# A two-layer hybrid diffusion backbone on one core: the convolution's output product gets its weights and two token operands in another way, and the layer heads order their norm and token sums anew

## The chip, the cores and the metric

The kernel runs on one core of a Trainium2 chip. The metric is the device time of one execution in microseconds, here the median of several runs. Before the change it is 2621.95 us (three runs, 2616.47 to 2628.95). A core has a matrix engine (TensorE, PE in the profile; its weight loads are shown as PEld), VectorE (DVE), ScalarE (ACT), GpSimd (POOL) and a queue engine SyncE (SP) that issues transfers. Each engine works through its own queue in order.

## The reference

Two layers over 1024 latent tokens of width 1024, with 256 context tokens that only the first layer reads. Layer 0 mixes tokens by bidirectional retention, layer 1 by a gated convolution of three taps; a SwiGLU block with 2816 hidden features follows each mixer. Every sub-layer is normed and modulated ahead and gated behind. Cut to what matters here (all of it float32):

```python
def rms_norm(x, gain=None):
    y = x * lax.rsqrt(jnp.mean(x * x, axis=-1, keepdims=True) + EPS)
    return y if gain is None else y * gain

def modulate(x, shift, scale):
    return x * (1 + scale) + shift

def conv_mixer(h, w_in, w_conv, w_out):
    b_gate, c_gate, xv = jnp.split(h @ w_in, 3, axis=-1)
    return (b_gate * short_conv(c_gate * xv, w_conv)) @ w_out

def swiglu(h, w1, w3, w2):
    return (jax.nn.silu(h @ w1) * (h @ w3)) @ w2

for i in range(2):
    sh1, sc1, g1, sh2, sc2, g2 = ada_params(c, ada_w[i], ada_b[i])
    ax = modulate(rms_norm(hx, norm_mix[i]), sh1, sc1)
    yx = retention_mixer(ax, ac, ...) if i == 0 else conv_mixer(ax, ...)
    hx = hx + g1 * yx
    fx = modulate(rms_norm(hx, norm_ffn[i]), sh2, sc2)
    hx = hx + g2 * swiglu(fx, ffn_w1[i], ffn_w3[i], ffn_w2[i])
return rms_norm(hx, final_norm)
```

## The kernel before, in words

**Precision.** Every large operand is held in two float32r parts, high and low. `split` makes them: ScalarE copies (rounds) the high part (L132, or L127 when the sign is turned), VectorE subtracts it from the source to get the low part (L133, or L128). `mm3` multiplies high by low, low by high and high by high into one bank of PSUM: three matmuls of 128 x 512 (L137 to L139). A pair of parts is one unit tile, from a pool of 38 that raw weight tiles of the same size share; single token tiles come from a pool of twelve (`ttile`) and one of twelve more (`ttile2`).

**Seven products.** Each weight matrix is multiplied by the tokens in a scheme of Strassen's kind (Winograd's form): weight and tokens are cut in halves both ways, and seven products of sums take the place of eight. Tokens are in two halves of 512 (`tb`), features in halves of four tiles of 128. x11, x12, x21, x22 are the quarters of the token matrix: first digit the half of the features, second digit the half of the tokens. Product 1 needs x11, product 2 x21, product 3 x22; products 5, 6, 7, 4 need sums: x12 - x11 and so on, in a chain. The tokens' sums are made in place; in the layers that widen, the norm's step already gives x12 and x21 the opposite sign, so that every step of the chain is an addition.

**Units.** In the layers that widen (`up_layer`, `winograd_products`) a unit is one product of one block of 128 output features: four feature tiles times three matmuls, twelve in all. In the layers that narrow (`down`) a unit is one product and one contraction tile for four output tiles, twelve matmuls again. The widening layers here are the feed-forward of layer 0, the convolution's input, the feed-forward of layer 1; the narrowing ones are the retention's output, the two feed-forward outputs and the convolution's output. The latter has four contraction tiles (`nh == 4`), hence 28 units, in the order of products 1, 5, 6, 3, 7, 4, 2. A widening layer starts with four blocks at once: product 1 of all four, product 2 of all four, then 5, 6, 7, 3, 4; after them the blocks follow one by one. Its first units, up to the start of product 5, are called its head.

**Order.** Work off TensorE is written as small functions in a list, `hooks`. After each unit `unit_done` takes one or more from the front; an entry `nothing` is a pause, which ends the turn. `until` takes hooks until an operand exists. What is written this way is a priority: a planner then puts the instructions on each engine's queue, in the written order unless in its own reckoning something behind is ready sooner. So the order in a queue can differ from the order in the text.

**The end of a narrowing layer and the head behind it.** `update` adds a finished bank times its gate to the residual (L1160, L1161 for a first result, L1164 for a second), `complete` squares it on ScalarE (L264) and sums the squares on VectorE (L265). `norm_steps` then does the norm: `diag` sums the squares over the partitions by eight tiny matmuls (L270) and takes the reciprocal root in small VectorE instructions (L275, L143 to L155), L288 builds a diagonal, and two matmuls spread it over the partitions (L296). Each of eight tiles is then scaled on VectorE (L1319) and shifted on ScalarE (L1321, L1323), by `modulator`, which also splits it where it is an operand. The early half of the tokens is normed during the last two products of the narrowing layer; the late half in the head of the next. There `run` of `up_layer` puts x12 into x11 and so on by accumulating transfers from GpSimd (`add`, L1348), around the last four scalings, and then splits the sums.

**Where the convolution's tokens come from.** `take` (in `x_steps`) gets each finished tile and stores the operands of the seven products to DRAM, products 1 to 3 from ScalarE's queue, the others from GpSimd's (L1281); sums of the chain are made on VectorE (L1294 to L1304). `down` loads them back on SP's queue (L1128), three ahead, and `operands` splits token tile and weight of a unit three units ahead. The weights come in halves (`w_load`, L1108); the second half of the first four blocks, and the accumulating transfer that adds a block to another (L1112), are asked for during product 1, that of the other block during product 6.

## Time and profile before

| | |
|---|---|
| median of the runs | 2621.95 us (2616.47 to 2628.95) |
| profiled execution | 2617.39 us, span 2615.5 us |
| TensorE busy | 2559.5 us, 98% |
| VectorE, ScalarE, GpSimd busy | 72%, 47%, 13% |
| mean granted TensorE clock | 0.994 |

Times in the profile are microseconds, `ns` where marked. A group row gives line, engine, operation, output and inputs, shape and count, then busy time, mean of one in ns, then the engine's idle time ahead of them and what ended it. A wait row gives who waited for whom, the total, how often, and the longest. A timeline row starts with start and length, and has the wait ahead in brackets. A window row has start and end, length, then the busy time and count of PE, PEld, DVE, ACT and POOL, the granted TensorE clock, the transfer engines' busy share and GB/s. Matmuls overlap, so their lengths add up to more than the time; their starts tell the pace.

### The profile page before, as it was taken

What the parts mean: (1) busy time and instruction counts of PE and PEld (TensorE: products, weight loads), DVE (VectorE), ACT (ScalarE), POOL (GpSimd) and SP (SyncE); (2) the same over time, 40 slices, a digit from 0 to 9 for tenths busy, and PEclk for the clock granted to TensorE, in tenths of its full rate; (3) what the DMA queues carried; (4) which work ended last, traced back from release to release, by engine and by line L of the source; (5) the groups of instructions that cost most, each with busy time, mean ns of one, the idle gap of its engine ahead of it and who ended that gap; (6) DMA issues with size and microseconds to landing.
All of it is one profiled execution on the core that took longest, in us unless ns stands there. A gap on an engine that the chain in (4) does not pass through costs nothing.

```text
span 2615.5 us, 33470 instructions
## 1 busy us (share of the span) xinstructions
PE 2559.5 (98%) x11508; PEld 2097.0 (80%) x11508; DVE 1891.9 (72%) x3349; ACT 1236.4 (47%) x2235; POOL 345.5 (13%) x434
## 2 busy tenths in 40 slices
PE   8999999999999999999999999999999999999998
PEld 4788788887777887888888888788777888887888
DVE  4887787775887878777775777877688666665766
ACT  4643343446766555433333545533365333333544
POOL 1101344001211202000001100200112000002100
PEclk9999999999999999999999999999999999999999
DMA  9546334855789956454557855432685333329733
GB/s 331 202 155 248 139 138 149 281 202 188 249 298 294 266 157 153 141 176 148 172 191 222 267 143 163 94 100 101 188 233 105 118 98 113 109 89 301 202 86 116
DMA packets 219627, 466.10 MB, mean 178 GB/s; under 512 B 23745, under 2 KB 53569, under 8 KB 219457
## 3 DMA queue, kind: packets, MB, share of 16 engines
q1 hardware_dynamic: 149232, 308.43, 36.4%
q0 software_dynamic: 39264, 100.16, 14.6%
q10 hardware_dynamic: 30960, 55.37, 5.7%
q8 instruction: 91, 1.49, 0.2%
q14 instruction: 80, 0.65, 0.1%
HBM read 331.22 MB, written 120.06 MB: 173 GB/s over the span
## 4 chain that ended last, share of the span: by engine, by line
PE 85%; DMA 5%; issue 4%; DVE 4%; ACT 1%; POOL 1%; SPq 0%; DVEq 0%; ACTq 0%; POOLq 0%
PE ps L137 28%; PE ps L138 28%; PE ps L139 28%; DVE u L133 1%; DMA raw<-in_w_kc 1%; DMA tt<-x_d 0%; PE ps L962 0%; DMA raw<-in_w 0%; DMA raw<-in_w_v 0%; DMA raw<-in_xT 0%; PE ps L743 0%; PE ps L270 0%; DVE tt L265 0%; DMA tt<-in_cxT 0%; PE ps L296 0%
## 5 line engine op out<-in xcount | busy, mean ns | idle before, releaser
L137 PE MATMUL ps<-u 128*128 128x512 f32 (+1 forms) x3492 | 1361.0, 390 | 22.7 <-DVE u L133 7.1
L138 PE MATMUL ps<-u 128*128 128x512 f32 (+1 forms) x3492 | 1354.2, 388 | 0.9 <-DVE u L133 0.9
L139 PE MATMUL ps<-u 128*128 128x512 f32 (+1 forms) x3492 | 1354.0, 388 | 0.0
L137 PEld LDWEIGHTS ps<-u 128*128 128x128 f32 x3492 | 657.8, 188 | 164.5 <-ACT u L132 11.1
L138 PEld LDWEIGHTS ps<-u 128*128 128x128 f32 x3492 | 658.4, 189 | 135.3 <-DVE u L133 2.5
L139 PEld LDWEIGHTS ps<-u 128*128 128x128 f32 x3492 | 658.3, 189 | 135.2 <-issue 0.7
L132 ACT CAST u<-raw 128x512 fp32r<-128x512 f32 x622 | 375.5, 619 | 363.3 <-PE ps L139 220.4
L133 DVE TENSOR_TENSOR u<-raw,u 128x512 fp32r<-128x512 f32 x622 | 436.5, 714 | 50.1 <-ACT u L132 48.1
L133 DVE TENSOR_TENSOR u<-tt,u 128x512 fp32r<-128x512 f32 x334 | 221.8, 687 | 117.6 <-ACT u L132 116.0
L132 ACT CAST u<-tt 128x512 fp32r<-128x512 f32 x334 | 198.2, 619 | 203.0 <-DMA tt<-x_d 88.8
L443 ACT COPY tt<-ps 128x512 f32<-128x512 f32 x192 | 112.6, 587 | 233.0 <-PE ps L139 224.0
L128 DVE SCALAR_TENSOR_TENSOR u<-raw,u 128x512 fp32r<-128x512 f32 x168 | 114.9, 688 | 76.6 <-ACT u L127 76.5
L127 ACT ACTIVATE u<-raw 128x512 fp32r<-128x512 f32 x168 | 105.0, 632 | 87.4 <-PE ps L139 75.8
L1281 POOL DMA_DIRECT2D x_d<-tt x52 | 28.3, 544 | 839.4 <-DVE tt L1294 819.0
L693 DVE SCALAR_TENSOR_TENSOR u<-ps,u 128x512 fp32r<-128x512 f32 x128 | 85.5, 687 | 38.5 <-ACT u L692 38.2
L456 DVE TENSOR_TENSOR tt<-tt,ps 128x512 f32<-128x512 f32 x64 | 43.8, 684 | 80.0 <-PE ps L139 79.8
L692 ACT ACTIVATE u<-ps 128x512 fp32r<-128x512 f32 x128 | 74.0, 598 | 34.1 <-PE ps L139 32.1
L450 DVE TENSOR_TENSOR tt<-tt,ps 128x512 f32<-128x512 f32 x64 | 43.9, 686 | 56.3 <-ACT tt L443 55.6
L210 DVE SCALAR_TENSOR_TENSOR raw<-raw,c_row 128x512 f32<-128x512 f32 x84 | 55.6, 687 | 21.3 <-DMA raw<-in_ada_t 21.1
L1164 DVE SCALAR_TENSOR_TENSOR t<-ps,ada,t 128x512 f32<-128x512 f32 x48 | 33.9, 748 | 50.0 <-PE ps L139 48.7
L635 POOL TENSOR_TENSOR u<-t,u 128x512 fp32r<-128x512 f32 x24 | 32.2, 1345 | 219.3 <-DMA t<-k_d 113.1
L133 DVE TENSOR_TENSOR u<-t,u 128x512 fp32r<-128x512 f32 x72 | 48.7, 687 | 15.8 <-ACT u L132 15.0
(174 smaller groups left out, 2134.6 us busy)
## 6 DMA issues: line engine op xcount, KB each, us to landing
tt<-x_d SPq DMA_DIRECT2D x182, 256.0 KB, 4.4
raw<-in_w SPq DMA_DIRECT2D x88, 512.0 KB, 4.1
raw<-in_w SPq DMA_DIRECT2D x88, 256.0 KB, 5.4
raw<-in_ada_t SPq DMA_DIRECT2D x42, 512.0 KB, 5.5
x_d<-tt ACTq DMA_DIRECT2D x78, 256.0 KB, 2.2
t<-in_ada_t SPq DMA_DIRECT2D x76, 256.0 KB, 6.1
raw<-in_w_v SPq DMA_DIRECT2D x36, 512.0 KB, 5.0
x_d<-tt POOLq DMA_DIRECT2D x52, 256.0 KB, 2.6
```

Of the source, the lines that this page charges most:

```text
L127: nc.scalar.activation(dst_hi, src, AF.Copy, scale=-1.0)
L128: nc.vector.scalar_tensor_tensor(dst_lo, src, -1.0, dst_hi.bitcast(F32), op0=ALU.mult, op1=ALU.subtract)
L132: nc.scalar.copy(dst_hi, src)
L133: nc.vector.tensor_sub(dst_lo, src, dst_hi.bitcast(F32))
L137: nc.tensor.matmul(ps, w_hi, x_lo, start=first, stop=False, **kw)
L138: nc.tensor.matmul(ps, w_lo, x_hi, start=False, stop=False, **kw)
L139: nc.tensor.matmul(ps, w_hi, x_hi, start=False, stop=last, **kw)
L210: nc.vector.scalar_tensor_tensor(w[e], w[e], 1.0, c_row[:, k], op0=ALU.mult, op1=ALU.mult, accum_out=sums[:, e, ct : ct + 1],)
L443: nc.scalar.copy(m[p, n], ps)
L450: nc.vector.tensor_add(t, t, banks[p, "c"])
L692: nc.scalar.activation(s[:, 0], st[d][m], AF.Copy, scale=f)
L693: nc.vector.scalar_tensor_tensor(s[:, 1], st[d][m], f, s[:, 0].bitcast(F32), op0=ALU.mult, op1=ALU.subtract,)
```

## The change

Nothing of the arithmetic's amount on TensorE changes. The parts:

1. **Widening layers.** Weights are made in order by `weights(end)`, and those of all eight first units (products 1 and 2 of four blocks) belong to the work listed ahead of the layer, not four of them. A turn behind these units takes four hooks, not two.
2. **Head.** The late half's norm has two pauses ahead of it. The first token sum (x12 into x11) is four additions on VectorE, and its splits for product 5 come next. The last four scalings follow, each with a transfer that adds the tile of x22 to x11 (product 6's operand). x22 is no longer split in `modulator`; product 3's splits come after product 7's. Product 4's operand is x21 plus the new x11.
3. **The convolution's output.** The second weight halves and the adding transfer are asked for in the list ahead (`w_rest`). The weights of products 4 and 2 are split by hooks during products 3 and 7 (`w_early`).
4. **The convolution's tokens of products 2 and 4** are split where they are made (`store_parts`: one ScalarE copy, one VectorE subtraction, two stores on GpSimd's queue) and stored as two parts, 512 KB; `down` loads them straight into a unit tile. The store for product 4 has two pauses of its own ahead.

```diff
-        ahead = [loads] + [lambda i=i: weight(i) for i in range(S_AHEAD)]
+        made = [0]
+
+        def weights(end):
+            while made[0] < end:
+                weight(made[0])
+                made[0] += 1
+
+        ahead = [loads] + [lambda i=i: weights(i + 1) for i in range(max(S_AHEAD, 2 * batch))]
...
-            weight(i + S_AHEAD)
+            weights(i + 1 + S_AHEAD)
...
-            unit_done(2 if i < steady and n in (1, 2) else 1)
+            unit_done(4 if i < steady and n in (1, 2) else 1)
...
+xp_d = spilled("xp_d", 2, KT // 2, shape=(P, 2, 512))
...
+        def w_rest(i):
+            w_load(i, 1)
+            w_load(nh + i, 1)
+            w_add(i)
...
-                xl[m] = ttile()
-                dst, x = xl[m], src(*seq[m])
-                if len(x.shape) == 3:
-                    dst = dst.rearrange("p (c t) -> p c t", c=4)
-                nc.sync.dma_start(dst, x)
+                x = src(*seq[m])
+                if x.shape[1] == 2:
+                    xl[m] = unit()
+                    nc.sync.dma_start(xl[m].bitcast(F32), x)
+                else:
+                    dst = xl[m] = ttile()
...
-            xs[m] = in_parts(xl.pop(m))
+            xs[m] = xl.pop(m)
+            if len(xs[m].shape) == 2:
+                xs[m] = in_parts(xs[m])
...
-            ws[m] = in_parts(t)
+            ws[m] = early.pop((n, i), None) or in_parts(t)
...
-            return [diag, nothing] + [lambda i=i, f=f: bank_of(i, f) for i, f in enumerate(consume(tb))]
+            wait = [nothing] * (2 if tb == order[0] else 0)
+            return wait + [diag, nothing] + [lambda i=i, f=f: bank_of(i, f) for i, f in enumerate(consume(tb))]
...
-        ahead += [lambda m=m: operands(m) for m in range(D_AHEAD)]
+        for m in range(D_AHEAD):
+            ahead.append(lambda m=m: operands(m))
+            if nh == 4:
+                ahead.append(lambda m=m: w_rest(m))
+        if nh == 4:
+            ahead.append(lambda: w_rest(3))
...
+        def w_early(n, i):
+            early[n, i] = in_parts(wr[nh + i][:, 512:] if n == 4 else wr[nh + i][:, :512])
...
+                    if n in (3, 7) and nh == 4:
+                        k = 4 if n == 3 else 2
+                        hooks.extend(lambda i=i, k=k: w_early(k, i) for i in range(nh))
...
-                if n == 1:
-                    w_load(i, 1)
-                    w_load(nh + i, 1)
-                    w_add(i)
+                if n == 1 and nh > 4:
+                    w_rest(i)
...
         def put(n, pr, t):
+            if n in in_two:
+                store_parts(xp_d[n // 4][pr], t, n == 4)
+                have.add((n, pr))
+                return
...
-                hooks.extend([nothing] * (4 if pr == 0 else 0) + [one, two])
+                late = [nothing, nothing, three] if 4 in in_two else []
+                hooks.extend([nothing] * (4 if pr == 0 else 0) + [one, two] + late)
...
-            if (i, j) != (0, 1):
-                x_parts(xc, {(0, 0): 1, (1, 0): 2, (1, 1): 3}[i, j], kt % 4, h)
+            if j == 0:
+                x_parts(xc, i + 1, kt % 4, h)
...
-            hooks.append(lambda: add(x11, x12))
-            hooks.extend(norms[-4:])
+            hooks.append(five)
+            hooks.extend(operands(5, x11))
+            for k in range(4):
+                hooks.append(norms[-4 + k])
+                hooks.append(lambda k=k: add(x11[k : k + 1], x22[k : k + 1]))
             hooks.append(lambda: add(x12, x22))
-            hooks.append(lambda: add(x22, x11))
-            hooks.append(lambda: add(x21, x22))
-            for n, x in ((5, x11), (6, x22), (7, x12), (4, x21)):
+            hooks.append(lambda: add(x21, x11))
+            for n, x in ((6, x11), (7, x12), (3, x22), (4, x21)):
                 hooks.extend(operands(n, x))
...
-    take, c_src = x_steps(KT // 2)
+    take, c_src = x_steps(KT // 2, (2, 4))
```

`five` adds the four tiles of x12 into x11 by `nc.vector.tensor_add`.

More of the change, by code (lines that the diff above doesn't have):

```diff
@@ L413, in loads, with winograd_products @@
                 load(p, 0)
-        ahead = [loads] + [lambda i=i: weight(i) for i in range(S_AHEAD)]
+        made = [0]
[4 more added lines that the diff above has]
+        ahead = [loads] + [lambda i=i: weights(i + 1) for i in range(max(S_AHEAD, 2 * batch))]
         return ahead, lambda *tail: winograd_products(
-            xc, blocks, tail, seq, ws, weight, order, also, steady
+            xc, blocks, tail, seq, ws, weights, order, also, steady
         )
-    def winograd_products(xc, blocks, tail, seq, ws, weight, order, also, steady):
+    def winograd_products(xc, blocks, tail, seq, ws, weights, order, also, steady):
         banks, m = {}, {}
@@ L1123, in x_loads @@
                     until(lambda: src(*seq[m]) is not None)
-                xl[m] = ttile()
-                dst, x = xl[m], src(*seq[m])
-                if len(x.shape) == 3:
-                    dst = dst.rearrange("p (c t) -> p c t", c=4)
-                nc.sync.dma_start(dst, x)
+                x = src(*seq[m])
[4 more added lines that the diff above has]
+                    dst = xl[m] = ttile()
+                    if len(x.shape) == 3:
+                        dst = dst.rearrange("p (c t) -> p c t", c=4)
+                    nc.sync.dma_start(dst, x)
                 loaded[0] += 1
@@ L1190, in down @@
         ahead[3:3] = [lambda: x_loads(D_LOADS)]
-        ahead += [lambda m=m: operands(m) for m in range(D_AHEAD)]
+        for m in range(D_AHEAD):
[4 more added lines that the diff above has]
+            ahead.append(lambda: w_rest(3))
+        early = {}
+        def w_early(n, i):
+            early[n, i] = in_parts(wr[nh + i][:, 512:] if n == 4 else wr[nh + i][:, :512])
         def step(ps, c, w, x, t, first, end):
@@ L1273, in h_of, with x_steps @@
         return h_d[kt][tb]
-    def x_steps(n_pairs):
+    def x_steps(n_pairs, in_two=()):
         parts, have = {}, set()
         def put(n, pr, t):
+            if n in in_two:
+                store_parts(xp_d[n // 4][pr], t, n == 4)
+                have.add((n, pr))
+                return
             (nc.scalar if n < 4 else nc.gpsimd).dma_start(x_d[n - 1][pr], t)
@@ L1304, in two, with three, src @@
                     nc.vector.tensor_sub(t4[0], x21, t2[0])
+                    if 4 not in in_two:
+                        put(4, pr, t4[0])
+                def three():
                     put(4, pr, t4[0])
-                hooks.extend([nothing] * (4 if pr == 0 else 0) + [one, two])
-        return take, lambda n, pr: x_d[n - 1][pr] if (n, pr) in have else None
+                late = [nothing, nothing, three] if 4 in in_two else []
+                hooks.extend([nothing] * (4 if pr == 0 else 0) + [one, two] + late)
+        def src(n, pr):
+            if (n, pr) in have:
+                return xp_d[n // 4][pr] if n in in_two else x_d[n - 1][pr]
+        return take, src
     def modulator(up, s, sh):
@@ L1351, in operands, with five @@
                 return [lambda kt=kt: x_parts(xc, n, kt, x[kt]) for kt in range(4)]
+            def five():
+                for d, t in zip(x11, x12):
+                    nc.vector.tensor_add(d, d, t)
             norms = [hooks.popleft() for _ in range(len(hooks))]
             hooks.extend(norms[:-4])
-            hooks.append(lambda: add(x11, x12))
-            hooks.extend(norms[-4:])
+            hooks.append(five)
[3 more added lines that the diff above has]
+                hooks.append(lambda k=k: add(x11[k : k + 1], x22[k : k + 1]))
             hooks.append(lambda: add(x12, x22))
-            hooks.append(lambda: add(x22, x11))
-            hooks.append(lambda: add(x21, x22))
-            for n, x in ((5, x11), (6, x22), (7, x12), (4, x21)):
+            hooks.append(lambda: add(x21, x11))
+            for n, x in ((6, x11), (7, x12), (3, x22), (4, x21)):
                 hooks.extend(operands(n, x))
```

## The prediction

> **What bounds the kernel now.** I read the page first, then TensorE's waits, then the stretches in which they lie, then those stretches instruction by instruction.
>
> ```profile
> span 2615.5 us, 33470 instructions
> PE 2559.5 (98%) x11508; PEld 2097.0 (80%) x11508; DVE 1891.9 (72%) x3349; ACT 1236.4 (47%) x2235; POOL 345.5 (13%) x434
> PE 85%; DMA 5%; issue 4%; DVE 4%; ACT 1%; POOL 1%; SPq 0%; DVEq 0%; ACTq 0%; POOLq 0%
> ...
> PE ps L270 <- DVE tt L265: 9.0, 4, 3.6
> ...
> PE ps L137 <- DVE u L133: 7.1, 5, 2.7
> ```
>
> TensorE is busy for 98% of the span and is 85% of the chain that ended last. The change takes no matmul away, so it can only give back time in which TensorE stands still or runs slowly. The waits it aims at are the norm's column sums (L270, waiting for the sum of squares at L265: 9.0 us, four times) and products that wait for splits (L137, of which 7.1 us for VectorE's half). Next, the stretches: three layer heads (eight products each up to the start of product five), the last eight units of the convolution's output, two units further ahead in it, and an undisturbed stretch for the price of a matmul.
>
> ```profile
> core 0: us, PE busy (x) PEld busy (x) DVE busy (x) ACT busy (x) POOL busy (x), PEclk, DMA share, GB/s
> 997.57:1027.46 29.89, 26.27 (x107) 21.23 (x106) 23.59 (x49) 18.29 (x32) 9.75 (x11) 0.89 0.53 113
> 1637.63:1663.12 25.49, 24.12 (x107) 19.13 (x106) 21.76 (x47) 16.24 (x29) 9.68 (x11) 1.00 0.60 122
> 1957.17:1988.89 31.72, 27.44 (x106) 21.80 (x107) 27.86 (x58) 21.79 (x39) 9.60 (x11) 0.89 0.54 114
> 1929.33:1957.17 27.84, 24.27 (x107) 18.94 (x105) 26.75 (x55) 18.42 (x33) 3.49 (x4) 1.00 0.78 234
> 1886.37:1896.64 10.27, 7.53 (x25) 5.53 (x24) 4.84 (x8) 5.34 (x10) 0.00 (x0) 0.84 1.07 312
> ...
> 1664.00:1864.00 200.00, 200.00 (x883) 165.47 (x882) 145.76 (x239) 78.64 (x135) 14.44 (x21) 1.00 0.35 102
> 1980.00:2040.00 60.00, 60.00 (x266) 49.67 (x266) 50.13 (x82) 32.78 (x59) 11.89 (x15) 1.00 0.56 129
> ```
>
> A 512-wide matmul costs 60.00/266 = 0.2256 us when nothing waits, so a unit of twelve costs 2.71 us and eight units 21.7. Inside the heads, TensorE's timeline (start, length, the wait ahead in brackets):
>
> ```profile
> 1004.07 1.86 PE L270 MATMUL ps<-ones,tt 128*128 128x1 f32 x8 [3.62 <-DVE tt L265]
> ...
> 1007.22 0.63 PE L137 MATMUL ps<-u 128*128 128x512 f32 x1
> 1007.64 0.63 PE L138 MATMUL ps<-u 128*128 128x512 f32 x1
> ...
> 1641.41 1.05 PE L270 MATMUL ps<-ones,tt 128*128 128x1 f32 x8 [0.90 <-DVE tt L265]
> 1642.32 0.48 PE L137 MATMUL ps<-u 128*128 128x512 f32 x1
> ...
> 1645.80 1.12 PE L296 MATMUL ps<-tt,ones 128*128 128x512 f32 x2 [0.47 <-DVE tt L288]
> 1646.37 0.80 PE L137 MATMUL ps<-u 128*128 128x512 f32 x1
> 1647.00 0.39 PE L138 MATMUL ps<-u 128*128 128x512 f32 x1
> ...
> 1891.96 0.47 PE L137 MATMUL ps<-u 128*128 128x512 f32 x1 [2.70 <-DVE u L133]
> ...
> 1953.04 0.70 PE L137 MATMUL ps<-u 128*128 128x512 f32 x2 [2.45 <-DVE u L133]
> ...
> 1957.17 0.50 PE L137 MATMUL ps<-u 128*128 128x512 f32 x1 [1.12 <-ACT u L132]
> 1958.54 0.50 PE L138 MATMUL ps<-u 128*128 128x512 f32 x1 [0.86 <-DVE u L133]
> ...
> 1964.73 1.66 PE L270 MATMUL ps<-ones,tt 128*128 128x1 f32 x8 [3.42 <-DVE tt L265]
> ```
>
> Eight column sums cost 0.91 us (1641.41 to 1642.32). The two spread matmuls cost 0.97 (1645.80 to 1647.00, less the one matmul between), with a wait of 0.47 ahead of them. A head without other waits is thus 21.7 + 0.9 + 1.0 + 0.5 = 24.0 us. Against it the feed-forward head at 997 is 5.9 us long, the convolution's head 1.5, the last feed-forward's head 7.7. The eight units from 1929.33 need 21.7 + 0.9 + 1.0 = 23.5 and take 27.84: 4.3 too many. All this is 19.4 us, the most these parts can give. The waits alone are less: behind the wait of 3.62 us the matmuls start 0.42 apart (1007.22, 1007.64) instead of 0.23, at a mean granted clock of 0.89 in that head; behind the 0.90 the clock stays at 1.00. So a long wait is paid nearly twice.
>
> The Trainium skill (TensorE: Matmul & The Clock Gate, Part 1: The HAM clock gate) says that the clock is halved after an idle window of about 3.4 us and comes back after about 3.4 us of work. Priced by that page (an estimate), the three L270 waits would be 3.62 + 0.90 + 3.42 and twice 1.7 for the slow stretch, 11.3 us instead of the 15.1 by the rows, and the sum below would be some 4 us smaller. The trace agrees on the halving, but not on the threshold: the head of the two units at 1886 has a wait of 2.70 only and yet a granted clock of 0.84.
>
> **The heads.** The norm of the later tokens gets two pauses, so two more units are ahead of the column sums: 5.4 us of matmuls against waits of 3.62 and 0.90. At the last head four weight splits are still queued, which use up one more unit's turn: 8.1 us against 3.42. These waits and their slow stretches go. What is late next is product five, whose tokens now come out of one chain on VectorE:
>
> ```profile
> 1642.50 0.16 DVE L275 TENSOR_SCALAR rs_v<-ps 128x4 f32<-128x4 f32 x1 [1.15 <-PE ps L270]
> ...
> 1644.88 0.87 DVE L288 TENSOR_SCALAR tt<-ident,rs_y 128x128 f32<-128x128 f32 x4
> 1646.97 2.73 DVE L1319 SCALAR_TENSOR_TENSOR tt<-tt,ada,ps 128x512 f32<-128x512 f32 x4 [1.22 <-PE ps L296]
> ...
> 1957.80 1.28 DVE L133 TENSOR_TENSOR u<-raw,u 128x512 fp32r<-128x512 f32 x2
> ...
> L446 DVE TENSOR_TENSOR tt<-tt,ps 128x512 f32<-128x512 f32 x64 | 43.8, 685 | 20.6 <-PE ps L139 20.3
> L1380 DVE TENSOR_TENSOR tt<-tt 128x512 f32<-128x512 f32 x66 | 45.2, 685 | 0.1
> L1348 POOL DMA_DIRECT2D t<-tt x12 | 10.7, 1104 | 56.9 <-ACT tt L1323 56.9
> ...
> t<-tt POOLq DMA_DIRECT2D x12, 256.0 KB, 4.7
> ```
>
> The norm's small instructions still take 1642.50 to 1645.75, 3.3 us against one unit of 2.71: the 0.47 wait stays and is in the 24.0. Behind the spread VectorE must scale four tiles (2.73), add four pairs (four at 0.60, the start to start of the L133 pair, 2.4) and split four (2.4): 7.5 us. Queued in between are three token adds of product two (L446, 0.69 each), one product of L1380 (0.69) and two weight splits (1.2): 11.4 in all. TensorE reaches the last quarter of product five's first unit 4 x 2.71 + 2.0 = 12.9 us after the spread's unit began, 12.3 after the scaling starts (0.6 later: 1646.97 against 1646.37). So two heads hold with 0.9 to spare. The last one has a unit less, 9.6, and is 1.8 short; of this some weight splits can go into VectorE's idle time before the norm, so I leave 1.5 of wait in. On the other side, the first sum no longer needs four accumulating transfers (1.10 us of GpSimd each, 4.7 to landing), and four splits of product three move behind product seven, out of the tight part; product six's sum is now made by transfers of 4.7 us that have four units (10.8 us) from there, so it is covered. If that cover is gone, each late tile is a wait of up to 4.7. The wider hook turns (four instead of two) only decide where this work is written, and cost nothing beside that. The weights of the first eight products are written earlier; the same splits, hidden in the stage before. Heads: 5.9 + 1.5 + (7.7 - 1.5) = 13.6 us.
>
> **The convolution's output, last eight units.** Today each unit needs a token tile and a weight split on both engines, and VectorE is busy for 26.75 of 27.84 us from 1929.33, with the modulation in between; the three waits there (2.45, 1.12, 0.86) are that queue. The change takes all sixteen pairs of splits out of these units: eight for tokens vanish, eight for weights move to earlier units. Sixteen at 0.60 are 9.6 us of VectorE time, twice the 4.3 that is lost. I take 4.0. What the moved work and the parts need elsewhere:
>
> ```profile
> 1910.00:1920.00 10.00, 10.00 (x46) 8.29 (x45) 4.36 (x7) 3.23 (x7) 1.16 (x2) 1.00 1.04 246
> ...
> L474 ACT CAST tt<-tt 128x512 fp32r<-128x512 f32 x20 | 12.4, 622 | 39.1 <-DVE tt L933 16.7 <-DVE tt L967 14.5 <-DVE tt L937 5.7
> L475 DVE TENSOR_TENSOR tt<-tt 128x512 fp32r<-128x512 f32 x20 | 18.1, 904 | 2.4 <-ACT tt L474 2.1
> x_d<-tt ACTq DMA_DIRECT2D x78, 256.0 KB, 2.2
> x_d<-t POOLq DMA_DIRECT2D x52, 256.0 KB, 4.1
> ```
>
> The eight moved weight splits are 4.8 us of VectorE, and between 1910 and 1920 it is free for 5.6 us: covered; if not, they are late by little, since products four and two come ten units later. Splitting the eight token tiles at the source costs eight times 0.62 us on ScalarE and 0.90 on VectorE (L474, L475), 5 and 7 us beside 121 and 54 us of idle time in the 200 us at 1664, where TensorE does not wait at all. Product two's store leaves ScalarE's queue (2.2 us to landing) and becomes two on GpSimd's (4.1), product four's one becomes two; SP then loads eight tiles of 512 KB instead of 256, 2.1 MB more at 246 GB/s: 8.5 us of transfer queues that are already at a share of 1.04. What gives way are the next layer's weight loads behind them on SP's queue, which are wanted from 1957 on, while 1929 to 1957 has a share of 0.78. I take nothing for it. The second weight halves asked for earlier stand in front of the token loads on SP's queue: two transfers fewer at the first units, so the wait of 2.70 before 1891.96 may shrink, but the last pair's products two and four now store two tiles' worth more through the same busy stretch (1.07). Its two units are 10.27 against 5.4, 4.9 too many. The change is bounded by -4.9 and, as much the other way, +4.9; I take 0: two loads fewer and two stores more, all of 256 KB, nearly cancel.
>
> **Sum.** 13.6 + 4.0 = 17.6 us. The profiled execution took 2617.39 around a span of 2615.5, 4.6 under the median of the three runs (2621.95). It becomes 2599.8, the median 2604.4.
>
> **Rivals.** (a) Product five late everywhere: VectorE's queue puts the other four scalings (2.73) ahead of the splits. 0.9 to spare becomes 1.8 short at two heads, the last is 4.2 short instead of 1.5 and, that long, brings a slow stretch like the first head's (5.9 less the wait of 3.62 is 2.3). That costs 1.8 + 1.8 + 2.7 + 2.3 = 8.6: 2613.0. For it: the order is set by a planner, not by the text alone. Against: the splits are written first. (b) The wait before 1891.96 goes too: 2599.5. For it speak the two loads fewer, against it the added stores. (c) It does not do what it says: the column sums stay directly behind the unit they stand behind now, since the planner places them, and only the last eight units gain: 2617.9. Against: they have no later unit ahead of them today that is written earlier. (d) Slower: the parts need two or one more of the twelve token tiles in the convolution, each held until its store lands. If each of the eight stores holds TensorE for its 4.1 us, 32.8 us are lost, 2637.2; it decides from 2.2 us a store, where the gain is eaten. Against it: no wait in the 200 us at 1664.
>
> **How the numbers follow.** My forecast 0.46 (2600 to 2609 by itself), (a) 0.21, (b) 0.14, (c) 0.12, (d) 0.07. The range, 2593 to 2620, holds all but (d) and the edges, with a few us for the runs' own spread. A measurement here tells about 0.5%, 13.1 us, from no change. Faster than 2608.8: 0.40 of the forecast, (b), and 0.06 of (a), 0.60. Slower: (d), 0.07. Same: 0.33.
>
> **What would show it.** Right: L270's waits for L265 near 1 us in all, granted clock near 1.00 in the three heads, about 24 to 26 us each; no L137 wait in the last eight units of the convolution's output, some 23.6 us. Wrong: an L137 wait for L133 at product five of each head (a); L270 directly behind the last output unit (c); any wait of TensorE in the convolution's products (d); a shorter or longer wait at the fourth unit of product five in the convolution's output (b). A gain in other stretches would mean that I left something out.

## The result, and the profile after

The changed kernel takes 2629.61 us in the median (14 runs, 2625.05 to 2633.96), the kernel before 2622.62 in the runs beside it (14 runs, 2616.47 to 2628.95). The ratio is 1.0026, with a 95% interval of 1.0019 to 1.0034: 7.0 us longer, where 17.6 less were forecast. It is within the 0.5% that the prediction called "same", but on the other side of the forecast, and the interval excludes no change.

First the page of the changed kernel: span, busy times, and the shares of the chain that ended last.

```profile
span 2628.3 us, 33496 instructions
PE 2560.3 (97%) x11508; PEld 2094.1 (80%) x11508; DVE 1901.1 (72%) x3361; ACT 1236.6 (47%) x2235; POOL 341.6 (13%) x434
PE 77%; DMA 7%; issue 6%; DVE 5%; ACT 2%; POOL 1%; SPq 1%; DVEq 0%; POOLq 0%; ACTq 0%
```

TensorE's work is the same, 11508 matmuls and weight loads. Its share of the chain fell from 85% to 77%. The engines are as busy as before, so this is a matter of waits. TensorE's waits in the changed kernel (who waited for whom, total, count, longest):

```profile
PE ps L137 <- DVE u L133: 19.3, 11, 4.1
...
PE ps L296 <- DVE tt L288: 6.8, 4, 4.4
...
PE ps L270 <- DVE tt L265: 1.1, 1, 1.1
```

The column sums (L270) waited 9.0 us before and wait 1.1 now: that part did what it says. In their place products wait 19.3 us for VectorE's half of a split (7.1 before), and the spread matmuls of the norm (L296) 6.8 us (2.0 before).

To see where, I cut both kernels into the same stretches, at the same matmul counted from the start of the program. Some stretches of the kernel before were shown in the prediction; these are the other four (a window row: start and end, length, busy time and count of PE, PEld, DVE, ACT, POOL, granted clock, transfer share, GB/s):

```profile
1027.46:1054.44 26.98, 26.98 (x121) 22.34 (x120) 22.04 (x36) 14.29 (x26) 4.35 (x5) 1.00 0.51 92
1663.12:1686.02 22.90, 22.90 (x103) 18.96 (x102) 18.86 (x31) 11.72 (x21) 4.42 (x6) 1.00 0.54 91
1870.04:1886.37 16.33, 16.33 (x73) 13.48 (x72) 15.02 (x27) 6.68 (x12) 5.89 (x8) 1.00 0.86 288
1988.89:2016.09 27.20, 27.20 (x121) 22.52 (x120) 21.96 (x36) 14.42 (x26) 4.51 (x6) 1.00 0.51 92
```

And the same view of the changed kernel, in order of time:

```profile
998.14:1022.47 24.33, 23.87 (x107) 19.21 (x106) 19.31 (x43) 11.89 (x20) 0.00 (x0) 1.00 0.16 52
1022.47:1051.97 29.50, 27.45 (x120) 22.18 (x119) 25.96 (x44) 19.90 (x36) 10.71 (x12) 1.00 0.73 135
1636.21:1660.56 24.35, 23.88 (x107) 19.21 (x106) 17.66 (x41) 11.14 (x19) 0.00 (x0) 1.00 0.12 44
1660.56:1685.57 25.01, 23.48 (x102) 18.80 (x101) 20.99 (x36) 14.99 (x27) 10.68 (x12) 1.00 0.76 126
1869.53:1892.17 22.64, 18.45 (x74) 14.65 (x72) 20.83 (x36) 13.12 (x24) 7.47 (x11) 0.92 0.78 251
1892.17:1897.61 5.44, 5.44 (x26) 4.50 (x24) 5.44 (x10) 3.40 (x8) 0.85 (x1) 1.00 1.09 264
1930.32:1956.08 25.76, 24.25 (x108) 19.09 (x107) 22.12 (x47) 14.82 (x26) 2.62 (x3) 1.00 0.68 217
1956.08:1988.95 32.87, 27.58 (x107) 21.26 (x107) 26.18 (x56) 16.37 (x30) 0.87 (x1) 0.90 0.29 76
1988.95:2023.91 34.96, 30.21 (x122) 24.06 (x121) 26.32 (x43) 20.22 (x36) 10.71 (x12) 0.90 0.65 127
```

Side by side, with the same stretches of e8 (below), the version that undid the harm. "Came" is the gain measured; a minus sign is a loss:

| stretch | before | after | forecast gain | came | corrected version (e8) |
|---|---|---|---|---|---|
| first feed-forward's head | 29.89 | 24.33 | 5.9 | 5.6 | 24.32 |
| products five and six behind it | 26.98 | 29.50 | 0 | -2.5 | 26.99 |
| convolution's head | 25.49 | 24.35 | 1.5 | 1.1 | 24.32 |
| products five and six behind it | 22.90 | 25.01 | 0 | -2.1 | 22.93 |
| convolution's output, start (two rows) | 26.60 | 28.08 | 0 | -1.5 | 22.56 |
| its last eight units | 27.84 | 25.76 | 4.0 | 2.1 | 25.06 |
| last head | 31.72 | 32.87 | 6.2 | -1.2 | 28.46 |
| products five and six behind it | 27.20 | 34.96 | 0 | -7.8 | 27.20 |
| sum | 218.62 | 224.86 | 17.6 | -6.2 | 201.84 |

The two profiled executions are 12.8 us apart, more than the medians (7.0), because before's is 5.2 below its median. Of the 12.8, 6.2 lie in these stretches and 4.7 behind 2023.91. There the changed kernel's execution has two more waits, 1.75 and 0.64 us (at 2406.40 and 2407.50), behind a load of a token tile that took 14.00 us. The kernels of e3, e5 and e8 have the same code there and do not show these waits, so I count the 4.7 as the spread of the runs. Each figure of the table is of one execution and has such a spread: e7, with the same code behind the first head, takes 32.31 us there (1022.92 to 1055.23), not 29.50.

The long waits of the changed kernel in these stretches, from TensorE's timeline:

```profile
1037.79 0.50 PE L137 MATMUL ps<-u 128*128 128x512 f32 x1 [2.05 <-DVE u L133]
...
1882.00 0.47 PE L137 MATMUL ps<-u 128*128 128x512 f32 x1 [4.15 <-DVE u L133]
...
1956.08 1.02 PE L137 MATMUL ps<-u 128*128 128x512 f32 x2 [1.28 <-ACT u L132]
...
1978.19 2.08 PE L296 MATMUL ps<-tt,ones 128*128 128x512 f32 x2 [4.37 <-DVE tt L288]
...
2004.48 0.50 PE L137 MATMUL ps<-u 128*128 128x512 f32 x1 [3.11 <-DVE u L133]
2007.08 0.79 PE L137 MATMUL ps<-u 128*128 128x512 f32 x1 [1.64 <-DVE u L133]
```

Three places remain to be explained: product six behind every head, the norm of the last head (4.37), and the start of the convolution's output (4.15).

**Product six.** Its tokens are x11 plus x22, added by accumulating transfers (L1394) as before, but now each behind a late scaling. First the kernel before at its last head, where the first of these transfers leaves 4.4 us ahead of product five's start (1988.89):

```profile
1984.49 0.87 POOL L1348 DMA_DIRECT2D t<-t  x1 [3.36 <-DVE tt L446]
```

Then the changed kernel, where product five starts at 1988.95: GpSimd's timeline (the first four `t<-t` add a tile of x22 to x11 for product six, `tt<-t` one of x22 to x12 for product seven, the later `t<-t` are for product four), how long these transfers of the last head were in flight (least, median, most), and a link of the chain that ended last:

```profile
1992.12 1.78 POOL L1394 DMA_DIRECT2D t<-t  x2 [30.50 <-ACT t L1367]
1993.47 2.22 POOL L1394 DMA_DIRECT2D tt<-t  x2
1994.64 1.96 POOL L1394 DMA_DIRECT2D t<-t  x1
1995.18 2.31 POOL L1394 DMA_DIRECT2D tt<-t  x1
1995.90 2.49 POOL L1394 DMA_DIRECT2D t<-t  x1
```

```profile
DMA to landing us min/median/max: 3.4/8.1/11.8
```

```profile
1995.90 9.76 DMA t<-t
2005.68 0.63 ACT u L132
```

The first transfer now leaves 3.2 us behind product five's start (1.1 and 2.4 at the other two heads, where it left 4.5 ahead before). The transfers leave within a few microseconds and land one behind the other: the first 3.4 us after its issue, at 1995.5; the seventh, issued at 1995.90, after 9.76 us. Product six's third and fourth tile are the fifth and seventh in that row, since those of product seven stand between them. TensorE was ready for the third tile at 2001.37 (2004.48 less 3.11); its split on ScalarE began at 2003.08, when it had landed. The fourth tile came at 2005.66. At the first head the chain is longer by a piece: the third tile lands 7.23 us after its issue at 1026.12, and three sums of weights (L396, L398) that stood behind its split in VectorE's queue come before the split that ends the wait of 2.05.

**The last head's norm.** VectorE's timeline, from the first small instruction behind the column sums to the diagonal (L288); of the rest only one of the large instructions in between is shown:

```profile
1970.96 0.16 DVE L275 TENSOR_SCALAR rs_v<-ps 128x4 f32<-128x4 f32 x1 [1.06 <-PE ps L270]
...
1972.61 0.69 DVE L396 TENSOR_TENSOR raw<-raw 128x512 f32<-128x512 f32 x1
...
1977.25 0.88 DVE L288 TENSOR_SCALAR tt<-ident,rs_y 128x128 f32<-128x128 f32 x4
```

From 1970.96 to 1978.13 are 7.2 us; at the convolution's head before it was 3.3. Eight instructions of some 0.69 us stand between the small ones of 0.16: two splits (L128), five sums of weights (L396, L398, L400) and a token add (L453). They are work for later that was put into the gaps of the chain; the small ones start some 0.2 us apart where nothing stands between them (1970.96 to 1971.77), and 0.7 us apart where one does.

**The start of the convolution's output.** ScalarE's timeline there, and SP's loads of token tiles (line 1145) in the same window with their time to landing:

```profile
1879.91 0.62 ACT L481 CAST tt<-t 128x512 fp32r<-128x512 f32 x1 [5.37 <-DVE t L1341]
1880.44 0.61 ACT L132 CAST u<-tt 128x512 fp32r<-128x512 f32 x1
```

```profile
L1145 SPq DMA_DIRECT2D tt<-x_d x7: 319/385/517, 1872.0 to 1881.3; - x7
...
DMA to landing us min/median/max: 2.7/2.9/4.8
```

ScalarE stood 5.37 us at the copy that makes the high part of product four's operand of the last pair (L481), because VectorE had not yet worked the chain up to it (L1341). Directly behind it in ScalarE's queue is the split of the token tile that TensorE needs. That tile was asked for at 1872.0 and there by 1876.8 even at the longest time to landing (4.8); it was split at 1880.44.

### The profile page after: what moved, and what is told of

Same layout as the page of the kernel before. It is cut to its first block, busy times and chain, and to the rows that moved or that the text cites. A ratio compares the mean times of both kernels' runs of the same rounds, so it can differ in the third digit from the quotient of the medians.

```text
span 2628.3 us, 33496 instructions
## 1 busy us (share of the span) xinstructions
PE 2560.3 (97%) x11508; PEld 2094.1 (80%) x11508; DVE 1901.1 (72%) x3361; ACT 1236.6 (47%) x2235; POOL 341.6 (13%) x434
## 4 chain that ended last, share of the span: by engine, by line
PE 77%; DMA 7%; issue 6%; DVE 5%; ACT 2%; POOL 1%; SPq 1%; DVEq 0%; POOLq 0%; ACTq 0%
PE ps L137 25%; PE ps L138 25%; PE ps L139 25%; DVE u L133 2%; PE ps L237 1%; DMA t<-t 1%; DMA tt<-os_d 1%; DMA u<-vp_d 1%; ACT u L132 1%; DMA raw<-in_w 1%; DMA tt<-x_d 1%; DMA raw<-in_w_v 1%; DMA t<-h_d 0%; PE ps L970 0%; DMA x_d<-tt 0%
## 5 line engine op out<-in xcount | busy, mean ns | idle before, releaser
L137 PE MATMUL ps<-u 128*128 128x512 f32 (+1 forms) x3492 | 1361.5, 391 | 35.3 <-DVE u L133 19.3
L128 DVE SCALAR_TENSOR_TENSOR u<-raw,u 128x512 fp32r<-128x512 f32 x168 | 115.5, 690 | 79.4 <-ACT u L127 79.2
```

The source lines that it names most:

```text
L128: nc.vector.scalar_tensor_tensor(dst_lo, src, -1.0, dst_hi.bitcast(F32), op0=ALU.mult, op1=ALU.subtract)
L137: nc.tensor.matmul(ps, w_hi, x_lo, start=first, stop=False, **kw)
```

## The experiments

My theory after these readings was that the loss lies in the heads (late transfers, stretched norm), with a new wait at the start of the convolution's output. The first rival put it in the convolution: the stores in two parts load the transfer queues. The two sides of the change were run apart. The runs of the kernel before beside these experiments have medians of 2621.14 (e1 to e4), 2622.43 (e5 to e8) and 2623.68 (e9, e10). Differences from the changed kernel are of plain medians below; measured from the kernel before beside each, they are up to 1.5 us smaller or larger.

**e1: heads alone.** All parts of the convolution's output undone.

```diff
-    take, c_src = x_steps(KT // 2, (2, 4))
+    take, c_src = x_steps(KT // 2)
-            if nh == 4:
-                ahead.append(lambda m=m: w_rest(m))
-        if nh == 4:
-            ahead.append(lambda: w_rest(3))
-                    if n in (3, 7) and nh == 4:
+                    if n in (3, 7) and nh == 0:
-                if n == 1 and nh > 4:
+                if n == 1:
```

> The changed kernel with its convolution-output parts undone (weights loaded and split as before, tokens stored in one part); the layer heads stay as changed. Theory A (the loss is made in the heads: the late norm's small instructions stand between full-size VectorE work at the last head, and product six waits for its transfers): the heads gain about 15.8 us at the column sums and lose about 6.7 at the spread, 12.3 at product six and 1.2 elsewhere, so this comes out at 2622.6 + 4.4 = about 2627, slower than the kernel before, with waits at product six in all three heads. Rival B (the stores and loads in two parts load the transfer queues, and that makes the loss): without them the heads' gain is left, about 2610 to 2615. Rival C (the loss sits in the starts of the output layers at about 860, 1415 and 2395 us, by chance of the run): the time scatters between 2618 and 2630 and does not hang on this part.

Measured: 2628.04 us, ratio to before 1.0028 (1.0017 to 1.0040).

**e2: convolution's output alone.** Pauses, eight weights ahead, the turn of four and the new order of sums undone.

```diff
-            wait = [nothing] * (2 if tb == order[0] else 0)
+            wait = []
-        ahead = ... range(max(S_AHEAD, 2 * batch))]
+        ahead = ... range(S_AHEAD)]
-            unit_done(4 if i < steady and n in (1, 2) else 1)
+            unit_done(2 if i < steady and n in (1, 2) else 1)
-            hooks.append(five)
...
+            hooks.append(lambda: add(x11, x12))
+            hooks.extend(norms[-4:])
...
```

> Only the convolution-output parts of the change; the layer heads as before. Theory A: the last eight units of that output gain 2 to 4 us, its start loses about 1.4, the column sums' waits are back (near 9 us in all): 2619 to 2622. Rival B: slower than the kernel before by 5 to 10 us, 2628 to 2632. Rival C: no difference that hangs on this part, 2622 with the same scatter.

Measured: 2621.98 us, ratio 1.0003 (0.9994 to 1.0011). With the heads' parts alone the kernel is as slow as with the whole change; the convolution's parts alone cost nothing. The rival falls: the doubled stores do not load the queues so that it can be seen. The second one (chance of the run at the starts of the output layers) falls too, since the two sides' times differ by 6 us. But these parts do not gain the forecast 4.0 either.

**e3: product six's sum on VectorE.** The transfers give way to four additions.

```diff
-                hooks.append(lambda k=k: add(x11[k : k + 1], x22[k : k + 1]))
+                hooks.append(lambda k=k: nc.vector.tensor_add(x11[k], x11[k], x22[k]))
```

> The changed kernel, with the sums for product six (x22 into x11, four tiles a head) made by VectorE additions in place of GpSimd's accumulating transfers. Theory A: the waits at product six (2.4, 2.1 and 7.8 us with their slow stretches) go, for 2.4 us more of VectorE a head: about 2618 to 2621; the wait of 4.4 at the last head's spread stays. Rival B and C: 2628 to 2630, as the changed kernel.

Measured: 2618.23 us, ratio 0.9989 (0.9979 to 0.9999), 11.4 below the changed kernel. The stretches with products five and six behind the three heads take 27.01, 22.90 and 31.26 us, against 29.50, 25.01 and 34.96. At the first two nothing is left of the loss. At the last 4 us are:

```profile
1982.35:2013.61 31.26, 29.12 (x122) 23.58 (x120) 28.65 (x47) 20.08 (x36) 7.14 (x8) 0.95 0.53 109
```

There the norm was still late (L296 waits 4.37 us in this kernel too), and with it the scalings that these sums need.

**e4: four weights ahead of a widening layer, not eight.**

```diff
-        ahead = ... range(max(S_AHEAD, 2 * batch))]
+        ahead = ... range(S_AHEAD)]
```

> The changed kernel, with four instead of eight weights listed ahead of a widening layer. Theory A: at the last head only two full-size VectorE instructions instead of eight stand in the norm's chain, so the spread's wait of 4.4 us falls to about 1 and its slow stretch goes: 6 us less, about 2623 to 2625; product six waits as in the changed kernel. Rival B and C: 2628 to 2630.

Measured: 2621.72 us, ratio 1.0002 (0.9992 to 1.0013), 7.9 below the changed kernel. The waits of the spread matmuls, and the last head with products five and six behind it:

```profile
PE ps L296 <- DVE tt L288: 3.8, 4, 1.4
```

```profile
1956.38:1984.87 28.49, 26.15 (x106) 20.45 (x107) 24.45 (x53) 15.85 (x28) 0.88 (x1) 0.94 0.30 72
1984.87:2018.20 33.33, 30.55 (x121) 24.40 (x120) 26.45 (x44) 20.06 (x35) 10.72 (x12) 0.90 0.66 126
```

In VectorE's timeline of this kernel only two splits (L128) stand inside the last head's chain of small instructions, and it is 28.49 long, not 32.87. Product six is still late: the transfers are untouched. So the norm and the transfers are two causes: e3 leaves the wait at the norm as it was, e4 the waits at product six (0.73 and 2.04 us). That the two together are the whole loss behind the heads, e8 shows.

**e5: no pauses ahead of the late norm.** The theory held that they cost more than they give, since product six's transfers are put off with the norm; the rival held that they only gain.

```diff
-            wait = [nothing] * (2 if tb == order[0] else 0)
+            wait = []
```

> The changed kernel without the two pauses ahead of the late tokens' norm. Theory A (the pauses move the column sums off the path, but push product six's transfers late by the same two units): the waits at the column sums come back (15.8 us with slow stretches), those at product six (12.3) and the long spread wait at the last head (6.7) go: 2629.6 + 15.8 - 19.0 = about 2626. Rival D (the pauses only gain, the lateness at product six has another cause, such as the ten wider hook turns): about 2640 to 2645.

Measured: 2631.60 us, ratio 1.0038 (1.0024 to 1.0053), 2.0 above the changed kernel, which is within the two intervals. Neither side's time came. The three heads:

```profile
999.33:1029.44 30.11, 26.49 (x107) 21.37 (x106) 23.61 (x49) 15.52 (x26) 6.43 (x9) 0.89 0.30 69
1644.95:1673.54 28.59, 27.02 (x107) 21.63 (x106) 21.14 (x46) 14.08 (x24) 5.12 (x7) 0.88 0.26 63
1970.77:2000.40 29.63, 26.21 (x107) 20.18 (x107) 26.29 (x56) 17.81 (x31) 4.25 (x7) 0.94 0.37 84
```

At the first two, without pauses, 5.8 and 4.2 us are lost again, and the column sums wait 3.62 and 1.57 us. At the last, 3.2 are gained, and 3.5 more behind it (31.47, not 34.96), where the transfers now start ahead of product five (1997.03 against 2000.40). So the pauses pay at the first two heads and are set off by the other faults at the last. Behind the first feed-forward's head TensorE is as late as with pauses (29.74 us against 29.50), but no longer for product six's tokens: their four transfers have landed by 1035.13, some 5 us ahead of product six's start at 1040.3, as the theory had it. The wait is now

```profile
1042.02 0.51 PE L137 MATMUL ps<-u 128*128 128x512 f32 x1 [1.46 <-ACT u L132]
```

and one of 0.65 behind it, both for the split of a weight. Its sums (L396) begin only at 1040.63, since VectorE's queue ahead of them stood 3.00 and 1.83 us for splits of token tiles that were still in flight. So the pauses do make the transfers late, and without them the transfers still hold TensorE up, by way of a queue.

**e6: the sums as before, the rest as changed.** It asks whether the old transfers would have done, with the later norm.

```diff
-            if j == 0:
-                x_parts(xc, i + 1, kt % 4, h)
+            if (i, j) != (0, 1):
+                x_parts(xc, {(0, 0): 1, (1, 0): 2, (1, 1): 3}[i, j], kt % 4, h)
...
-            hooks.append(five)
-            hooks.extend(operands(5, x11))
...
+            hooks.append(lambda: add(x11, x12))
+            hooks.extend(norms[-4:])
+            hooks.append(lambda: add(x12, x22))
+            hooks.append(lambda: add(x22, x11))
+            hooks.append(lambda: add(x21, x22))
```

> The changed kernel with the token sums of the heads as before: the first sum by transfers, product three's splits in the norm step, product six from x22 plus x11. Pauses, weights ahead and turns stay as changed. Theory A: with the pauses the transfers of the first sum and of the one behind it are two units later than before, so product five and six both wait in each head, two to four us each and more at the last: 2628 to 2636. Rival E (VectorE's sum and its place are what makes product six late): product six no longer waits, about 2616 to 2620.

Measured: 2637.17 us, ratio 1.0057 (1.0043 to 1.0071), a little above what was expected and 7.5 above the changed kernel. Now the first sum is late as well: product five waits 1.56 us at the first feed-forward's head, 1.55 at the convolution's and 3.98 at the last. With the old transfers product five is late once the norm is put off; e6 undoes the whole new order with the addition, so it does not show the addition's share alone.

**e7: the last pair's operand of product four in one part.** It asks whether ScalarE's stand at L481 makes the wait of 4.15 us.

```diff
-            if n in in_two:
+            if n in in_two and (n, pr) != (4, n_pairs - 1):
                 store_parts(xp_d[n // 4][pr], t, n == 4)
...
-                late = [nothing, nothing, three] if 4 in in_two else []
+                late = [nothing, nothing, three] if 4 in in_two and pr < n_pairs - 1 else []
```

> The changed kernel, with the last pair's token operand of product four stored in one part again, so that no ScalarE copy waits for the end of the sums' chain in front of the first splits of the convolution's output. Theory F (that copy blocks ScalarE's queue for 5.4 us while a landed token tile waits behind it, and TensorE stands for 4.1 us at about 1878): the wait goes, and with the earlier weights the old wait of 2.7 near 1892 does not come back: 4 to 6 us less, about 2624 to 2626. Rival G (the tile is late for its transfers): the wait stays or moves on, 2628 to 2630.

Measured: 2624.11 us, ratio 1.0005 (0.9995 to 1.0015), 5.5 below the changed kernel. The stretch that took 22.64 us in the changed kernel:

```profile
1872.45:1889.57 17.12, 17.12 (x73) 13.28 (x72) 16.28 (x30) 10.22 (x18) 6.95 (x10) 1.00 0.72 239
```

TensorE does not wait in it, at a clock of 1.00 instead of 0.92. The edit also takes away the pauses ahead of that store and one of its two transfers, but ScalarE's timeline of e7 shows what mattered: the first split of the convolution's output (1877.63) waits 0.19 us, for the landing of its tile and for nothing else. One copy in the wrong place of a queue was the cause.

**e8: e3, e4 and e7 together.**

> Three corrections at once: product six's sums on VectorE (11.4 us less by itself), four weights ahead (7.9 less by itself), the last pair's product four in one part (theory F: 5 less). If they add up, of 2629.6 some 24 go: 2605 to 2608, faster than the kernel before by 0.5 to 0.6%. If the first two take away the same wait at the last head, 2610 to 2613.

Measured: 2604.47 us (five runs, 2604.23 to 2604.79), ratio 0.9932 (0.9920 to 0.9944). That is 25.1 below the changed kernel, where the three alone sum to 11.4 + 7.9 + 5.5 = 24.8; measured from the kernel before beside each it is 25.0, and the three sum to 21.6. Either way no gain is counted twice: the causes are separate. It is 0.68% below the kernel before, the best of all. Two of its stretches, behind the first and the last head (the others are in the column on the right of the table above):

```profile
1024.95:1051.94 26.99, 26.99 (x120) 22.28 (x119) 26.96 (x46) 19.07 (x35) 7.14 (x8) 1.00 0.52 98
...
1975.60:2002.80 27.20, 27.20 (x121) 22.52 (x120) 27.15 (x46) 18.22 (x33) 7.14 (x8) 1.00 0.52 98
```

Behind the heads VectorE is busy for 26.96 of 26.99 and 27.15 of 27.20 us, and yet TensorE does not wait. VectorE has no idle time left there: another sum in these stretches would put other work off, and no run shows what that would cost.

**e9 and e10: what the two sides are worth in e8.** e9 takes the pauses from it (edit as in e5), e10 all parts of the convolution's output (edit as in e1).

> The combined version (four weights ahead, product six's sum on VectorE, last pair's operand for product four in one part) without the two pauses ahead of the late norm. Theory: the pauses carry the gain of the heads once nothing late stands behind them; without them the column sums wait again, 3.6 us with a slow stretch at the first feed-forward head (5.8 in all by the prediction's stretches), 0.9 to 1.6 at the convolution's head, up to 3.4 at the last: 2611 to 2616. Rival: the run of the changed kernel without pauses came only 2 us above it, so the pauses are worth about 2 here too: 2604 to 2607.

> The combined version with all parts of the convolution's output undone (weights asked for and split as before, tokens in one part). Theory: storing product four's last operand in two parts was the only harm in those parts (5.5 us); with it gone they are worth what the last eight units gained, 3 to 5 us, so undoing them gives 2607.5 to 2610. Rival: they only move the wait and are worth nothing: 2603.5 to 2605.5. The waits in the last eight units of the convolution's output (2.45, 1.12, 0.86 in the kernel before) are back in either case.

Measured, beside 2623.68 for the kernel before on that chip: e9 2614.87 us, ratio 0.9970 (0.9958 to 0.9981); e10 2615.90 us, ratio 0.9971 (0.9960 to 0.9981). So the pauses are worth some 9 to 10 us where nothing late is behind them, as the theory had it, against 2 in the changed kernel; the heads of e9 are 4.7, 2.0 and 3.0 us longer than those of e8. The convolution's parts are worth 10 to 11, more than either side expected. The rows of e10 for the two units around the old wait of 2.70, the last eight units and the last head say why:

```profile
1883.81:1894.19 10.38, 7.16 (x26) 5.26 (x24) 4.60 (x8) 5.09 (x10) 0.00 (x0) 0.88 1.08 312
...
1927.31:1954.94 27.63, 24.02 (x107) 19.02 (x105) 26.45 (x55) 18.11 (x33) 3.50 (x4) 1.00 0.73 226
1954.94:1986.52 31.58, 27.80 (x107) 21.46 (x107) 25.42 (x55) 16.14 (x28) 0.00 (x0) 0.89 0.14 42
```

Against e8 the start of the convolution's output is 4.2 us longer (26.72, not 22.56; a wait of 3.18), the last eight units 2.6, and the last head 3.1: its norm chain is filled again with work that the fuller queue of the last units has left over (L296 waits 3.42). This last part I had not counted to the convolution's output at all.

## Why the prediction was wrong, step by step

**Which waits bind: right.** The gains came in the stretches that the prediction looked at. Most of the loss, 12.4 us, lies in stretches that it did not cut out, products five and six behind each head. The column sums' waits went from 9.0 to 1.1 us, the first two heads take 24.33 and 24.35 us at a clock of 1.00 ("about 24 to 26 us each"), and their gain, 6.7 us, is near the forecast 7.4. Rival (c) falls.

**Product five in time: right.** TensorE waits nowhere at product five's tokens in the changed kernel. The 0.9 us to spare held at two heads; rival (a) falls. With the old sums (e6) product five waits at all three heads.

**Product six covered: wrong, the largest fault.** The step was: "product six's sum is now made by transfers of 4.7 us that have four units (10.8 us) from there, so it is covered". Two terms of it failed, the start and the length. The transfers do not leave when product five starts: they stand behind the late norm, product five's additions and its splits, and the fourth leaves 4.3, 7.4 and 7.0 us after that start at the three heads. At the last one this leaves 10.8 + 2.0 - 7.0 = 5.8 us to the last quarter of product six's first unit, of which its splits on both engines take 1.4 (2005.68 to 2007.08); the 4.4 that are left are not enough even for the 4.7. And the 4.7 was read from the row of product five's transfers (`t<-tt`). Those that add `t` to `t`, for products six and four, had another row, here of the kernel before and of the changed one:

```profile
t<-t POOLq DMA_DIRECT2D x24, 256.0 KB, 6.0
```

```profile
t<-t POOLq DMA_DIRECT2D x24, 256.0 KB, 8.3
```

In the changed kernel ten leave within 6 us at the last head, in an order that mixes two products, and they land one after another, so the fourth tile needs 9.76. The stretches behind the heads are 2.5, 2.1 and 7.8 us longer, 12.4 in all; e3 gives 11.4 back by the medians, 8.3 of it in these stretches. The prediction did name the price ("each late tile is a wait of up to 4.7") and then set it to nothing.

**The norm takes 3.3 us: wrong at the last head.** "The norm's small instructions still take 1642.50 to 1645.75, 3.3 us against one unit of 2.71: the 0.47 wait stays". The duration was taken from a head whose VectorE queue had nothing to put in between. At the last head the chain takes 7.2 us, TensorE waits 4.37 and then runs slowly: the head loses 1.2 us where 6.2 gained were forecast. Beside it stood "The weights of the first eight products are written earlier; the same splits, hidden in the stage before". They are not: e4, which makes four of them ahead as before, brings that head to 28.49 (its chain takes 4.2 us) and the whole down by 7.9. What was priced as moved work at no cost put its successors into the most critical chain.

**The start of the convolution's output: a size taken by cancelling.** The prediction bounded it by 4.9 either way and took 0, "two loads fewer and two stores more". Came 1.5 lost, and inside the bounds, but not by transfers: the old wait went altogether (its two units take 5.44, not 10.27, a gain of 4.8), and a new one of 4.15 us came four units ahead, from ScalarE's queue. The prediction counted the split at the source as 0.62 us of an idle ScalarE. The instruction's length was right; that it waits at the head of an engine's queue, with a split that TensorE needs behind it, was not asked. Without that (e7, e8) the start gains 4.0. Rival (b) saw the gain; the new wait hid it.

**The last eight units: right in kind, too large.** 2.1 us in the changed kernel and 2.8 in e8, not 4.0. The wait of 2.45 is gone. The 1.28 ahead of the next layer's first matmul (1.12 before) stays: it is for the weights of that layer's first product, which the change does not move past the modulation on ScalarE. Nor does the 0.86 go that the prediction counted with them and that lies just behind, in the last head: it is 0.90 in the changed kernel and in e8. Even in e8 that head takes 28.46 us, 4.5 over its 24.0, with this wait, 1.42 at the spread and a clock of 0.94; that accounts for most of the 3.6 by which the heads fall short of their 13.6 in e8.

**Rival (d), parts holding TensorE in the convolution's products: falls.** The stretch between has no wait and is as long as before, 183.96 us for the same matmuls at a clock of 1.00:

```profile
1685.57:1869.53 183.96, 183.96 (x812) 152.06 (x811) 137.38 (x227) 74.11 (x129) 14.97 (x25) 1.00 0.36 118
```

None of the rivals was the one that came, a transfer and a queue late behind the wait that was removed. With the three faults undone, e8 lands 0.1 us from the forecast; but by its own terms that is partly chance: heads 10.0 for 13.6, last eight units 2.8 for 4.0, and 4.0 at the start of the convolution's output where nothing was counted.

**Still open:** why ten accumulating transfers land so far apart (their issue order was not varied), how the loss behind the heads divides between their late start and their long flight (e3 takes both away), and why one load took 14.00 us in the changed kernel's execution.

## What to carry to other kernels

Where a stall is removed by putting a step off, walk on from there until every consumer of that step has been met, with the issue and landing of each transfer in a row rather than the median of one. A move that adds no work can still cost: ask of every moved instruction what stands behind it in its engine's queue while it waits, and what long instructions may be put between short ones of a critical chain. When a combined change disappoints, run its sides and single steps apart: here three small edits turned 0.3% slower into 0.7% faster, with the change's idea left as it was.

## What the runs showed of the hardware that was not expected

**Accumulating transfers of 256 KB, issued one after another, land in a row**: seven of them took from 1995.5 to 2005.66, some 1.7 us from one landing to the next, with times in flight from 3.4 to 11.8 us. The Trainium skill (DMA: Bandwidth & Descriptors, Anatomy of one DMA) gives a fixed 2.0 us and the bytes at 436 GB/s, an estimate of 2.6 us for one of these and 0.6 us for each one behind it; the trace does not agree on either.

**How long a wait must be to bring a slow stretch is not fixed.** The matmuls behind the 2.05 us at 1037.79 of the changed kernel keep their pace (that stretch has a granted clock of 1.00), those behind 2.14 us in e3 do not. The first row is e3 from the end of that wait, the second the kernel before from the end of its wait of 2.45:

```profile
1995.53:1999.00 3.47, 3.47 (x8) 2.72 (x9) 3.47 (x6) 2.88 (x6) 0.00 (x0) 0.52 1.10 190
```

```profile
1953.04:1957.17 4.13, 3.01 (x12) 2.14 (x12) 4.13 (x7) 4.13 (x9) 1.75 (x2) 1.00 0.46 99
```

Eight matmuls in 3.47 us are half pace, twelve in 3.01 are full pace, after the longer wait. In the traces of all these kernels every wait of TensorE from 2.70 us up in these stretches was followed by a slow stretch, and of those from 1.5 to 2.6 some were. The price does not grow with the wait: where a slow stretch came, the 40 matmuls behind it took some 1.5 to 3.3 us more than the 9.02 of full pace (40 times 0.2256), 10.82 after the 2.14 us of e3 and 11.21 after the 4.37 of the changed kernel. So "paid nearly twice" holds for waits of 2 to 3 us, and is too much for 4.4. The Trainium skill (TensorE: Matmul & The Clock Gate, Part 1) has the clock halved after an idle window of about 3.4 us, and calls the window free-running; the second fits these rows, the first as a bound on one wait does not. Such waits may also make the runs' spread: the five runs of e8, which has no wait above 1.42 us in these stretches, lie within 0.6 us, the 14 of the kernel before within 12.5. No run tests this.
